# Two attention steps of the first tile moved by one product each, and two of four groups of weight sums formed at the second tile's begin

## The chip, the cores and the metric

The kernel runs on one core of a Trainium2 chip. TensorE (PE) multiplies matrices, VectorE (DVE) and ScalarE (ACT) do elementwise work, GpSimd (POOL) does masks here and issues some DMAs, SyncE (SP) issues most DMAs. Each engine works through its own instructions in order and waits on semaphores for the others. The metric is the device time of one execution in microseconds; lower is better.

## The reference

One layer of a hybrid decoder block on x of 1 x 2048 x 1024 in float32:

```
h = rms_norm(x, norm_g);  u = h @ w_in          # 8704 columns, cut into nine parts
y_c = b_c * conv3(c_c * v_c) * silu(z_c);       y_a = y_c @ w_conv_out
q, k = rms_norm per head (16 and 4 heads of 64)
o = attention(q, k, v, sinks) * silu(z_a);      y_b = o @ w_attn_out
merged = sigmoid(g_a + b) * y_a + sigmoid(g_b + b) * y_b
out = x + merged @ w_out
```

The attention looks back 128 positions, in blocks of 128, and each query head has a learned sink that takes part in the softmax.

## The kernel before, in words

**Tiles and products.** The 2048 positions are worked on in two tiles of 1024 (tile 0 and tile 1), weights on the partitions, positions along the free axis in halves of 512. A projection is cut into units. Each unit (`sunit`, L650) computes a 2 x 2 block of results with seven block products instead of eight, from sums and differences of the blocks of weights and of activations. Every value is held as a rounded high part and a low part, so a product is 4 x 3 = 12 matmuls of 128x128 by 128x512 (`product`, L633; the matmul is L639). The order of the products of a unit is 1, 5, 6, 2, 7, 3, 4: the first fills a bank `X`, which ACT copies to the bank `Y`; the second fills `V`; the third adds into `Y`; then DVE adds `Y` and the kept copy `s5` of `V` into `V`, and only after that the fifth product (weights `th`, `tl`) may go on writing `Y`.

**What sets the order.** All engines run in the order in which the program was written (a manual schedule). The function `run` takes one product after the other and counts them in `tick`; `put(n, f)` places a piece of other work right behind product n. So a number in one of the tables at the head of the file is the number of a product, and one product is the unit in which work is moved. Tile 1 runs k, v, four units of q, eight of conv inputs with four of b, the gates ga and gb, four of z, four of za, then the output projections.

**Attention.** One step is one group of four query heads and one block of 128 queries; there are 32 in a tile, numbered 0 to 31 (step r has key head r // 8 and block r % 8). Step r is placed by STEPS_0[r] for tile 0 and STEPS_1[r] for tile 1, a product number n: SP loads the operands (n - 5, for three late steps n - 6), ACT puts the sinks as a column into the bank of scores (`att_bank` L1237, n - 2), PE forms the scores `s` (L1249 and L1252, n), ACT the exponentials `p` (L1274, n + 1), DVE normalises (n + 2) and transposes within 32 x 32 squares into `f` (n + 2), POOL stores that to HBM (`fd`, L1293) and loads it back in another order (`x`, four DMAs, L1300, n + 4), ACT rounds it to `xh` and `yp` (n + 9), DVE forms the low part `xl` (n + 10) and POOL masks with four selects (L1321, n + 10), PE multiplies with the values into `po` (L1338, n + 13, for two steps n + 14), ACT and DVE sum `po` into `o` (up to n + 15), and SP stores it (`od`, L1358). There is one bank of scores in all.

**Weight sums of w_out.** `wo_sums(n, j)` (L1595) forms for one of four groups of 256 rows of `w_out` the four differences that the last projection needs: behind product n SP loads two pieces of 512 KB into the two buffers of the pool `u` (`wos`, L1601); from n + 5 to n + 7 DVE does four subtractions of 128x512 and SP stores each result of 256 KB in HBM (`wsd`, L1606). They are read again much later. The two `u` buffers serve other loads too, but one group fills both, so a group's loads wait for the stores of the group before it.

**Queues.** SP's DMAs take eight semaphores in turn, and a DMA waits until the one issued eight before it has landed. POOL's DMAs do the same with eight of their own. A wait in such a queue holds all that stands behind it.

Of the kernel before, what the change touches and what calls it, by code (L numbers as in the profile page):

```python
# [27 lines left out]
KP = KC // 2  # L28
# [45 lines left out]

CSUM_AT = (2, 14, 12, 20)
CONV_AT = (3, 0, 0, 0, 1, 2, 3, 8, 8, 4, 7, 8, 5, 11, 9, 2, 5, 9, 11, 12, 15, 16, 15, 17, 14, 12, 11, 13)
WO_SUMS_AT = (8, 17, 26, 35)
WO_AHEAD = 3
THS_AT = 10
HOLD = 10  # L80
STEPS_0 = (60, 63, 71, 74, 78, 85, 92, 95, 99, 104, 110, 115, 121, 128, 131, 136, 139, 142, 146, 149, 152, 155, 159, 162, 165, 170, 173, 176, 181, 184, 187, 192)
STEPS_1 = (53, 57, 63, 69, 72, 77, 84, 87, 93, 98, 104, 111, 114, 118, 125, 129, 132, 136, 139, 142, 145, 148, 153, 158, 161, 164, 168, 171, 175, 178, 181, 184)
Z_AHEAD = (7, 4)
SUM_WAIT = 5
# [41 lines left out]
def block_kernel(  # L126
# [13 lines left out]
    NT = S // T  # L140
# [48 lines left out]
    def hs(q):  # L189
        return slice(q * H, (q + 1) * H)  # L190
# [121 lines left out]
    def sub(o, a, b, eng=None):  # L312
        return (eng or vec).tensor_tensor(out=o, in0=a, in1=b, op=ALU.subtract)
# [568 lines left out]
    tick = [0]  # L882
    at = {}

    def put(n, f):
        at.setdefault(max(n, tick[0] + 1), []).append(f)
# [306 lines left out]
    def att_load(t, j, b):  # L1193
        nm = f"{t}_{j}_{b}"
        gb = t * NB + b
        kz = lows[(j * NB + b) % 2]
        q2 = slot([P, 2, 2, P], F32R, f"q2_{nm}")
        nc.sync.dma_start(
            q2.bitcast(F32).rearrange("p h c x -> p (h c x)"),
            q2d[t][j][:, 2 * b : 2 * b + 2].rearrange("p h c e x -> p (h c e x)"))  # L1200

        kq = slot([P, 2, 2 * P], F32R, f"kq_{nm}")
        for c in range(2):
            nc.sync.dma_start(
                kq[HALVES[c], 1].bitcast(F32).rearrange("p (h x) -> p h x", h=2),
                q2d[t][j][LH, 2 * b : 2 * b + 2, c].rearrange("p h e x -> p h (e x)"))

        blocks = [(t, b - 1, 0, 2)] if b else [(t, 0, 1, 1)]
        if b == 0 and gb > 0:
            blocks.append((t - 1, NB - 1, 0, 1))  # L1210
        for kt, k0, to, n in blocks:
            here, there = slice(to * P, (to + n) * P), slice(k0 * P, (k0 + n) * P)
            nc.sync.dma_start(kq[:, 0, here].bitcast(F32), kd[kt][j, :, 0, there])
            for c in range(2):
                nc.sync.dma_start(kz[HALVES[c], c, here].bitcast(F32), kd[kt][j, HALVES[c], 1, there])
        return q2, kq, kz

    def att_load_v(t, j, b):

        v2 = slot([P, 4, P], F32R, f"v2_{t}_{j}_{b}")
        hb = (t * NB + b) * 2
        v4 = v2.bitcast(F32).rearrange("p n d -> p (n d)")
        src = vd[j, :, hb : hb + 4].rearrange("k n d -> k (n d)")
        nc.sync.dma_start(v4[UH], src)

        pairs = src[:, 0 : 2 * P].unsqueeze(1).to_broadcast([HD, 2, 2 * P])
        (rows, _, cols_) = pairs.ap  # L1230
        pairs = bass.AP(pairs.tensor, pairs.offset, [rows, [P, 2], cols_])
        nc.sync.dma_start(v4[LH].rearrange("p (i x) -> p i x", i=2), pairs)
        return v2

    def att_bank(t, j, b):
        sp = ps_s.tile([P, 2, 2, 2 * P], F32, tag="s", name=f"s{t}_{j}_{b}")
        nc.scalar.copy(sp[:, :, :, 3 * HD : 3 * HD + 1], sinks_of[t, j][:, b // HB, b % HB].unsqueeze(3))  # L1237
        return sp

    def att_scores(t, j, b, ld, sp):  # L1240
        first = t * NB + b == 0
        nm = f"{t}_{j}_{b}"
        q2, kq, kz = ld
        rv = rqs[t, j][:, b // HB, b % HB]
        for h in range(2):
            skip = (2 - h) * HD if first else 0
            keys = slice(h * HD + skip, (h + 3) * HD)
            for c in range(2):
                nc.tensor.matmul(  # L1249
                    sp[:, h, c, skip : 3 * HD], lhsT=q2[:, h, c, :], rhs=kq[:, 0, keys],  # L1250
                    start=c == 0, stop=False)
            nc.tensor.matmul(  # L1252
                sp[:, h, :, skip : 3 * HD], lhsT=kq[:, 1, h * P : (h + 1) * P], rhs=kz[:, :, keys],
                start=False, stop=True)
        sg = sp.rearrange("p h c k -> p (h c) k")
        m = mask_i.unsqueeze(1).to_broadcast([P, G, HD])
        if first:
            vec.copy_predicated(
                sg[:, :, 2 * HD : 3 * HD], m, negc.unsqueeze(1).to_broadcast([P, G, HD]))
            vec.tensor_copy(sg[:, 0:2, HD : 2 * HD], negc.unsqueeze(1).to_broadcast([P, 2, HD]))  # L1260
        else:
            vec.copy_predicated(sg[:, :, 2 * HD : 3 * HD], m, sg[:, :, 0:HD])
        st = small.tile([P, 3, G], F32, tag="st", bufs=4, name=f"st{nm}")
        vec.tensor_reduce(out=st[:, 0], in_=sg[:, :, HD : 3 * HD + 1], axis=AX.X, op=ALU.max)
        vec.scalar_tensor_tensor(
            out=st[:, 1], in0=st[:, 0], scalar=-1.0, in1=rv.rearrange("p h c -> p (h c)"),
            op0=ALU.mult, op1=ALU.mult)
        return sg, st, rv

    def att_exp(t, j, b, got):  # L1270
        sg, st, rv = got
        p = slot([P, G, P + 1], F32, f"p{t}_{j}_{b}")
        for i in range(G):
            nc.scalar.activation(  # L1274
                out=p[:, i, :], in_=sg[:, i, HD : 3 * HD + 1], func=AF.Exp, bias=st[:, 1, i : i + 1],
                scale=rv[:, i // 2, i % 2 : i % 2 + 1], accum_out=st[:, 2, i : i + 1])
        return p[:, :, 0:P], st
# [317 lines left out]
    def wo_sums(n, j):  # L1595
        two = []

        def ld():
            for i in range(2):
                u = upool.tile([P, 2 * H + 2], F32, tag="u", name=f"wos_{j}_{i}")  # L1600
                nc.sync.dma_start(u[:, 0 : 2 * H], w_o[(2 * j + i) * P : (2 * j + i + 1) * P, :])  # L1601
                two.append([u[:, hs(q)] for q in range(2)])

        def out(m, a, b, c):
            sub(a, b, c)
            nc.sync.dma_start(wsd[m, j], a)  # L1606

        put(n, ld)
        put(n + SUM_WAIT, lambda: out(0, two[0][0], two[0][1], two[0][0]))
        put(n + SUM_WAIT + 1, lambda: out(1, two[0][1], two[1][1], two[0][1]))  # L1610
        put(n + SUM_WAIT + 1, lambda: out(2, two[1][1], two[1][1], two[0][0]))
        put(n + SUM_WAIT + 2, lambda: out(3, two[1][0], two[1][0], two[1][1]))
# [57 lines left out]
    for n in range(S // P // 2):  # L1670
        t, c0 = divmod(2 * n * P, T)
# [204 lines left out]
    def attention(t, places):  # L1876
        for r, n in enumerate(places):
            j, b = divmod(r, NB)
            got = {}

            def step(k, f, got=got):
                def g():
                    got[k] = f(got)
                return g

            put(n - 5 - ((t, r) in EARLY_LOADS), step("l", lambda g, j=j, b=b: att_load(t, j, b)))
            put(n + V_, step("v", lambda g, j=j, b=b: att_load_v(t, j, b)))
            put(n - 2, step("k", lambda g, j=j, b=b: att_bank(t, j, b)))
            put(n, step("s", lambda g, j=j, b=b: att_scores(t, j, b, g["l"], g["k"])))
            put(n + 1, step("e", lambda g, j=j, b=b: att_exp(t, j, b, g["s"])))  # L1890
            put(n + 2, step("n", lambda g: att_norm(g["e"])))
            put(n + F_, step("f", lambda g, j=j, b=b: att_flip(t, j, b, g["n"])))
            put(n + B_, step("b", lambda g, j=j, b=b: att_back(t, j, b, g["f"])))
            put(n + X_, step("x", lambda g, j=j, b=b: att_turn(t, j, b, g["b"])))
            put(n + L_, step("w", lambda g: att_low(g["x"])))
            late = int((t, r) in VALUES_LATER)
            put(n + late + O_, step("o", lambda g, j=j, b=b: att_values(t, j, b, g["w"], g["v"])))
            put(n + late + O_ + 1, step("z", lambda g, j=j, b=b: att_out(t, j, b, g["o"])))
            put(n + late + S_, step("t", lambda g, j=j, b=b: att_sum(t, j, b, g["z"])))
# [56 lines left out]
    for t in range(NT):  # L1956
# [5 lines left out]
            t0 += T0_SHIFT  # L1962


        attention(t, [t0 + n for n in (STEPS_0, STEPS_1)[t]])
        if t > 0:
            run(sunit(("k", t), ops, fin_k(t)))
# [25 lines left out]
        zs += [("za", j) + fin_z(t, j, od[t], "za", use_y) for j in range(NJ)]  # L1993
        zs[0][3]()
        if t + 1 == NT:
            for j in range(KP):
                wo_sums(tick[0] + WO_SUMS_AT[j], j)
        if t == 0:
            for j in range(2):
# [151 lines left out]
```

## Time and profile before

| what | value |
|---|---|
| median of 3 runs | 1901.33 us (1898.82 to 1902.93) |
| the profiled execution, its own time | 1901.07 us |
| its span, first to last instruction | 1899.4 us |
| PE busy | 1888.9 us, 99% |
| PE weight loads | 1572.7 us, 83% |
| DVE busy | 1498.6 us, 79% |
| ACT busy | 990.5 us, 52% |
| POOL busy | 608.7 us, 32% |
| granted TensorE clock | 1.000 |
| HBM traffic | 271.09 MB read, 129.25 MB written |

In the rows of a timeline stand the start and the length in microseconds, the engine, the line, the operation, what it writes and reads, the shapes, how many instructions were put together, and in brackets the idle time of the engine before it with what ended it. Matmuls overlap, so a row of 0.61 us of two matmuls does not fill as much time: twelve of them follow each other in 2.7 us. In tile 0 the last attention steps lie between about 545 and 630 us; tile 1 begins near 890 us, its q units run from 928 to 1004 us, its z units start at 1432 us.

### The profile page before, as it was taken

The numbers are of one execution on the slowest core, as the hardware profiler recorded it, in microseconds if no ns is written. First come the engines' busy times: TensorE is split into PE (matmuls) and PEld (weight loads), VectorE is DVE, ScalarE is ACT, GpSimd is POOL, SyncE is SP. The second block draws the span as 40 slices with busy tenths as digits, with TensorE's granted clock in tenths as the row PEclk, the third lists the DMA queues.
The fourth block names the chain that finished last, engine by engine and source line by source line (L and its number), as shares of the span: only waits on it lengthen the run. The fifth ranks groups of instructions, "written<-read, shape, count | busy, mean of one in ns | idle before, by whom it ended". The sixth has DMA issues, their size and how long they took to land.

```text
span 1899.4 us, 27260 instructions
## 1 busy us (share of the span) xinstructions
PE 1888.9 (99%) x8670; PEld 1572.7 (83%) x8670; DVE 1498.6 (79%) x2364; ACT 990.5 (52%) x1967; POOL 608.7 (32%) x846
## 2 busy tenths in 40 slices
PE   9999999999999999999999999999999999999999
PEld 7888888888887888888888888888888888888887
DVE  7989898887777767668799788887778777787754
ACT  7665455456766443434565455556666434444321
POOL 2073435335655000011372344445656000121000
PEclk9999999999999999999999999999999999999999
DMA  8286555568777957895584655567778887779653
GB/s 299 77 238 177 167 169 167 162 189 245 240 229 226 302 197 245 276 279 130 155 233 128 181 175 154 168 206 228 242 235 256 272 319 274 274 194 264 215 175 110
DMA packets 222495, 402.20 MB, mean 212 GB/s; under 512 B 30032, under 2 KB 104784, under 8 KB 212880
## 3 DMA queue, kind: packets, MB, share of 16 engines
q1 hardware_dynamic: 188224, 313.10, 50.6%
q0 software_dynamic: 30528, 78.94, 15.7%
q10 hardware_dynamic: 3600, 8.42, 1.3%
q8 instruction: 69, 1.13, 0.2%
q14 instruction: 74, 0.61, 0.1%
HBM read 271.09 MB, written 129.25 MB: 211 GB/s over the span
## 4 chain that ended last, share of the span: by engine, by line
PE 65%; DVE 2%; DMA 2%; issue 0%; ACT 0%; SPq 0%; DVEq 0%; ACTq 0%
PE Y L639 24%; PE ya L1479 4%; PE Vcv L639 2%; PE Xcv L639 2%; PE Xyb L639 2%; PE Vo L639 2%; PE Xo L639 2%; PE Vyb L639 2%; PE Vza L639 2%; PE Xza L639 2%; PE Xz L639 1%; PE Vz L639 1%; PE po L1338 1%; PE Vga L639 1%; PE Xgb L639 1%; PE Vgb L639 1%
## 5 line engine op out<-in xcount | busy, mean ns | idle before, releaser
L1300 POOL DMA_DIRECT2D x<-fd x256 | 140.0, 554 | 127.0 <-DMA fd<-f 58.1
L1274 ACT ACTIVATE p<-s,st,rq 128x129 f32<-128x129 f32 x256 | 114.2, 458 | 33.2 <-DVE st L275 21.2
L1321 POOL TENSOR_SCALAR_AFFINE_SELECT xh<-xh 64x512 fp32r<-64x512 f32 x64 | 61.0, 953 | 151.4 <-DVE xl L275 103.2
L1293 POOL DMA_DIRECT2D fd<-f x64 | 37.0, 578 | 194.3 <-DVE f L275 169.0
L1562 POOL DMA_DIRECT2D mt<-tha x16 | 13.8, 863 | 254.9 <-DVE tha L275 236.2
L639 PE MATMUL Xcv<-oph,wcv_ah 128*128 128x512 f32 x256 | 78.9, 389 | 0.0
L1321 POOL TENSOR_SCALAR_AFFINE_SELECT yp<-xl 64x512 fp32r<-64x512 f32 x64 | 72.3, 1130 | 3.1
L1321 POOL TENSOR_SCALAR_AFFINE_SELECT xl<-xl 64x512 fp32r<-64x512 f32 x64 | 67.7, 1058 | 4.4
L1321 POOL TENSOR_SCALAR_AFFINE_SELECT yp<-yp 64x512 fp32r<-64x512 f32 x64 | 57.8, 903 | 4.2
L275 DVE TENSOR_TENSOR o<-po,o 64x256 f32<-64x256 f32 x128 | 53.5, 418 | 5.0 <-ACT o L1350 4.1
L275 DVE SCALAR_TENSOR_TENSOR y<-u,cols,y 128x512 f32<-128x512 f32 x64 | 53.6, 837 | 3.7 <-ACT y L1387 2.5
L639 PEld LDWEIGHTS Xcv<-oph,wcv_ah 128*128 128x128 f32 x256 | 47.8, 188 | 9.4
L275 DVE TENSOR_TENSOR p<-p,st 128x512 f32<-128x512 f32 x64 | 50.4, 787 | 3.4
L275 DVE STREAM_TRANSPOSE f<-p 128x512 f32<-128x512 f32 x64 | 45.5, 711 | 8.5 <-DMA fd<-f 5.6
L466 ACT CAST wcv_sh<-wcv_raw 128x1024 fp32r<-128x1024 f32 x16 | 16.9, 1054 | 67.1 <-DVE wcv_raw L275 67.1
L1274 ACT ACTIVATION_READ_ACCUMULATOR p<-s,st,rq 128x1 f32 x256 | 51.3, 200 | 0.0
L1249 PEld LDWEIGHTS s<-kq,q 128*128 128x128 f32 x256 | 46.1, 189 | 5.8 <-ACT s L1237 1.8
L1078 POOL DMA_DIRECT2D q2d<-q_h x64 | 44.3, 692 | 18.9 <-ACT q_h L1073 7.7
L1350 ACT COPY o<-po 64x256 f32<-64x256 f32 x128 | 47.1, 368 | 6.0 <-DMA wpd_yb<-wph_yb 2.2
L2052 POOL DMA_DIRECT2D oc<-ocd x12 | 6.5, 545 | 136.1 <-ACT ophc L306 130.1
L639 PE MATMUL Xcv<-oph,wcv_al 128*128 128x512 f32 x128 | 49.9, 390 | 0.0
L1078 POOL DMA_DIRECT2D q2d<-q_l x64 | 44.2, 690 | 14.7 <-DMA q2d<-q_h 7.5
(711 smaller groups left out, 6409.1 us busy)
## 6 DMA issues: line engine op xcount, KB each, us to landing
gd<-th SPq DMA_DIRECT2D x64, 256.0 KB, 2.8
wcv_raw<-in_w_units SPq DMA_DIRECT2D x16, 1024.0 KB, 5.5
q<-q2d SPq DMA_DIRECT2D x64, 256.0 KB, 5.4
v<-vd SPq DMA_DIRECT2D x128, 128.0 KB, 3.5
fd<-f POOLq DMA_DIRECT2D x64, 256.0 KB, 4.2
x<-fd POOLq DMA_DIRECT2D x256, 64.0 KB, 3.5
th<-gd SPq DMA_DIRECT2D x48, 256.0 KB, 5.0
wga_raw<-in_w_units SPq DMA_DIRECT2D x8, 1024.0 KB, 5.4
```

What stands on the lines that cost most here:

```text
L275: r = f(*args, **kw)
L466: return (lambda: nc.scalar.copy(hi, src), lambda: vec.tensor_tensor(out=lo, in0=src, in1=hi.bitcast(F32), op=ALU.subtract))
L639: nc.tensor.matmul(ps, lhsT=w[:, j, :], rhs=b[:, m, :], start=start and j == 0 and i == 0, stop=j == KP - 1 and i == 2, skip_group_check=n ...
L1078: nc.gpsimd.dma_start(q2d[t][j][half, q * 2 * HB : (q + 1) * 2 * HB, i, e, :], src[HALVES[e]].bitcast(F32).rearrange("p (b x) -> p b x", x ...
L1249: nc.tensor.matmul(sp[:, h, c, skip : 3 * HD], lhsT=q2[:, h, c, :], rhs=kq[:, 0, keys], start=c == 0, stop=False)
L1274: nc.scalar.activation(out=p[:, i, :], in_=sg[:, i, HD : 3 * HD + 1], func=AF.Exp, bias=st[:, 1, i : i + 1], scale=rv[:, i // 2, i % 2 : i ...
L1293: nc.gpsimd.dma_start(fd, f)
L1300: nc.gpsimd.dma_start(x[QUADS[k]], src[k])
L1321: nc.gpsimd.affine_select(out=d4, in_=s4, pattern=[[0, 2], [-32 * sg, 2], [0, G], [-sg, 32]], compare_op=ALU.is_gt if prev else ALU.is_ge, ...
L1338: nc.tensor.matmul(po[:, cs], lhsT=v2[:, kind + h, :], rhs=xx[:, :, h * HD : (h + 1) * HD], start=n == h == 0, stop=n == 2 and h == 1)
L1350: nc.scalar.copy(ov, pov[oth, :, e])
L1479: nc.tensor.matmul(ps, lhsT=w[:, j, cs], rhs=o[:, m, :], start=n == 0 and i == 0, stop=n == KC - 1 and i == 2)
```

## The change

Two tables and one loop are changed. In STEPS_0 step 28 comes one product earlier (181 to 180) and step 30 one product later (187 to 188); the last five steps then stand at 176, 180, 184, 188 and 192. The four groups of w_out's sums were all placed from the first z unit of tile 1 on, behind its products 8, 17, 26 and 35. Now groups 0 and 1 are placed from tile 1's begin on, behind products 5 and 13 (in k's and v's units), and groups 2 and 3 from the first z unit on, behind products 8 and 44.

```diff
-WO_SUMS_AT = (8, 17, 26, 35)
+WO_SUMS_AT = (5, 13, 8, 44)
...
-STEPS_0 = (..., 170, 173, 176, 181, 184, 187, 192)
+STEPS_0 = (..., 170, 173, 176, 180, 184, 188, 192)
...
+        if t + 1 == NT:
+            for j in range(2):
+                wo_sums(tick[0] + WO_SUMS_AT[j], j)
         attention(t, [t0 + n for n in (STEPS_0, STEPS_1)[t]])
...
         if t + 1 == NT:
-            for j in range(KP):
+            for j in range(2, KP):
                 wo_sums(tick[0] + WO_SUMS_AT[j], j)
```

On POOL, at the end of tile 0's attention, before the change (`3_2`, `3_3` and `3_4` are steps 26, 27 and 28; the last number is the buffer's):

```order
L1300 DMA x_3_3_5716<-fd_3_3_5653 32x4x128 x4
L1321 AFFINE_SELECT xh_3_2_5771<-xh_3_2_5771 64x512
L1321 AFFINE_SELECT yp_3_2_5773<-yp_3_2_5773 64x512
L1321 AFFINE_SELECT yp_3_2_5773<-xl_3_2_5772 64x512
L1321 AFFINE_SELECT xl_3_2_5772<-xl_3_2_5772 64x512
L1293 DMA fd_3_4_5821<-f_3_4_5819 128x512
L1300 DMA x_3_4_5894<-fd_3_4_5821 32x4x128 x4
L1321 AFFINE_SELECT xh_3_3_5886<-xh_3_3_5886 64x512
```

The same place in the changed kernel:

```order
L1300 DMA x_3_3_5716<-fd_3_3_5653 32x4x128 x4
L1293 DMA fd_3_4_5777<-f_3_4_5775 128x512
L1321 AFFINE_SELECT xh_3_2_5768<-xh_3_2_5768 64x512
L1321 AFFINE_SELECT yp_3_2_5770<-yp_3_2_5770 64x512
L1321 AFFINE_SELECT yp_3_2_5770<-xl_3_2_5769 64x512
L1321 AFFINE_SELECT xl_3_2_5769<-xl_3_2_5769 64x512
L1300 DMA x_3_4_5849<-fd_3_4_5777 32x4x128 x4
L1321 AFFINE_SELECT xh_3_3_5894<-xh_3_3_5894 64x512
```

Step 28's store now stands ahead of step 26's four selects; its loads stay between the selects of steps 26 and 27.

On SP, in k's, v's and q's units of tile 1 (`wq` are q's weights, `krd` and `krb` the store and the spread loads of the keys' scales), before:

```order
L437 DMA wq_0_raw<-in_w_units 128x2048
L437 DMA wq_1_raw<-in_w_units 128x2048
L1143 DMA krd_104<-krt_8938 32x32 x4
L1152 DMA krb_0_0_8980<-krd_104 64x512 x2
L437 DMA wq_2_raw<-in_w_units 128x2048
L1152 DMA krb_1_1_9036<-krd_104 64x512 x2
```

and in the changed kernel:

```order
L437 DMA wq_1_raw<-in_w_units 128x2048
L1606 DMA wsd<-wos_0_8764 128x512 x2
L1606 DMA wsd<-wos_1_8766 128x512 x2
L1143 DMA krd_104<-krt_8950 32x32 x4
L1601 DMA wos_0_8977<-in_w_out 128x1024
L1601 DMA wos_1_8979<-in_w_out 128x1024
L1152 DMA krb_0_0_8996<-krd_104 64x512 x2
L437 DMA wq_2_raw<-in_w_units 128x2048
L1152 DMA krb_1_1_9052<-krd_104 64x512 x2
L1152 DMA krb_0_1_9102<-krd_104 64x512 x2
L1606 DMA wsd<-wos_0_8977 128x512 x2
```

The first group's loads stand ahead of the rows shown, its stores ahead of `krd`; the second group's two loads now stand between `krd` and the first `krb`.

On DVE, between q's first and second unit of tile 1, in the changed kernel:

```order
L275 SCALAR_TENSOR_TENSOR q_0_0_0_l<-q_0_0_0_t,gqk,q_0_0_0_h 128x512
L275 TENSOR_TENSOR wos_0_8977<-wos_0_8977 128x512
L275 TENSOR_TENSOR k_1_1_t<-k_1_1_t,krb_1_1_9052 128x512
L275 TENSOR_TENSOR wq_1_d<-wq_1_raw,wq_1_d 128x512
L275 TENSOR_TENSOR q_0_1_1_t<-Y,s5q_0_9083 128x512
L275 TENSOR_TENSOR wos_0_8977<-wos_1_8979,wos_0_8977 128x512
L275 TENSOR_TENSOR wos_1_8979<-wos_1_8979,wos_0_8977 128x512
L275 TENSOR_TENSOR k_1_1_l<-k_1_1_t,k_1_1_h 128x512
```

Before, the three `wos` rows were not there and the others followed each other; the group's fourth subtraction comes five rows further on. All four stand ahead of the second unit's `Vq`.

More of the change, by code (lines that the diff above doesn't have):

```diff
@@ L80 @@
 HOLD = 10
-STEPS_0 = (60, 63, 71, 74, 78, 85, 92, 95, 99, 104, 110, 115, 121, 128, 131, 136, 139, 142, 146, 149, 152, 155, 159, 162, 165, 170, 173, 176, 181, 184, 187, 192)
+STEPS_0 = (60, 63, 71, 74, 78, 85, 92, 95, 99, 104, 110, 115, 121, 128, 131, 136, 139, 142, 146, 149, 152, 155, 159, 162, 165, 170, 173, 176, 180, 184, 188, 192)
 STEPS_1 = (53, 57, 63, 69, 72, 77, 84, 87, 93, 98, 104, 111, 114, 118, 125, 129, 132, 136, 139, 142, 145, 148, 153, 158, 161, 164, 168, 171, 175, 178, 181, 184)
```

## The prediction

> **What bounds the kernel now.** I read the page first, then the waits of TensorE (PE), then the chain of waits around each of them, then the timelines of the engines named there.
>
> ```profile
> span 1899.4 us, 27260 instructions
> ...
> PE 1888.9 (99%) x8670; PEld 1572.7 (83%) x8670; DVE 1498.6 (79%) x2364; ACT 990.5 (52%) x1967; POOL 608.7 (32%) x846
> ```
>
> TensorE is busy for all but 10.5 us of the span. The change removes no matmul, so only those idle microseconds are to be won, while a new pause of TensorE is lost whole. The waits of TensorE (line, who released it, us in total, times, longest) say where they are:
>
> ```profile
> PE s L1249 <- ACT s L1237: 1.4, 1, 1.4
> ...
> PE po L1338 <- POOL yp L1321: 0.8, 1, 0.8
> PE Y L639 <- DVE zs L275: 0.8, 1, 0.8
> PE po L1338 <- DMA gd<-th: 0.6, 1, 0.6
> PE po L1338 <- POOL xl L1321: 0.3, 1, 0.3
> ```
>
> The two `po` waits on POOL and the `s` wait lie among the last attention steps of tile 0, the `Y` wait in tile 1's z stage, where w_out's sums are formed. They make 0.8 + 0.3 + 1.4 + 0.8 = 3.3 us, or 0.17% of the time: all that the change can win.
>
> **Attention, first wait.** In POOL's timeline (start, length, idle time and its releaser in brackets), with two rows of VectorE (DVE) and two of PE:
>
> ```profile
> 562.14 1.31 POOL L1321 TENSOR_SCALAR_AFFINE_SELECT xh<-xh 64x512 fp32r<-64x512 f32 x1 [3.70 <-DVE st L275]
> ...
> 566.76 0.58 POOL L1293 DMA_DIRECT2D fd<-f  x1
> 573.49 2.19 POOL L1300 DMA_DIRECT2D x<-fd  x4 [6.14 <-issue]
> 575.68 0.76 POOL L1321 TENSOR_SCALAR_AFFINE_SELECT xh<-xh 64x512 fp32r<-64x512 f32 x1
> ...
> 579.16 0.58 POOL L1293 DMA_DIRECT2D fd<-f  x1
> ```
> ```profile
> 562.86 0.71 DVE L275 STREAM_TRANSPOSE f<-p 128x512 f32<-128x512 f32 x1
> ...
> 583.33 0.71 DVE L275 STREAM_TRANSPOSE f<-p 128x512 f32<-128x512 f32 x1 [3.40 <-DMA fd<-f]
> ```
> ```profile
> 578.42 0.51 PE L1338 MATMUL po<-yp,v 128*128 128x256 f32 x2 [0.79 <-POOL yp L1321]
> ...
> 589.33 0.47 PE L1249 MATMUL s<-kq,q 128*128 128x192 f32 x2 [1.37 <-ACT s L1237]
> ```
>
> The reader sees POOL finish step 26's four selects (562.14 to 566.8), issue step 28's store `fd`, stand still until that has landed, issue its four loads `x`, and only then begin step 27's selects at 575.68, for which TensorE waits at 578.42. One product of twelve matmuls takes 2.72 us:
>
> ```profile
> 599.33 2.72 PE Y L639 x12
> ```
>
> With step 28 one product earlier its `f`, now at 562.86, comes at best at 562.86 - 2.72 = 560.1, inside POOL's idle 3.70 us; its store stands ahead of step 26's selects now. The landing (566.76 to 573.49, 6.7 us) then runs beside them: 560.2 + 6.7 = 566.9. DVE does step 28's three operations first, about 1.6 us (0.71 for the transpose, the rest from it by size), so the selects end at some 568.4, the loads are issued by 570.6, and step 27's selects begin 5 us earlier than 575.68. TensorE's wait needs 1.1 of that: **-1.11** (0.79 and 0.32). Should `f` not come earlier at all, the store goes out at 563.6, the selects follow, and step 27's begin at about 572: enough too. If DVE's reordering eats more, the wait stays: bounds -1.11 and 0.
>
> **Second wait.** Step 29's store goes out at 579.16 because it stands behind step 27's selects. Step 30's transpose waits until 583.33 for a slot that this store holds; behind it DVE is late for weights, ScalarE (ACT) for a cast, and behind that cast in ACT's order the sink column of step 31 is late, for which TensorE waits 1.37 at 589.33. All that comes 5 us earlier, while step 30 itself is one product later and its transpose stands behind that weight work. **-1.37**; if the single bank of scores, which step 30 now holds a product longer, is free too late, 0.
>
> **What is late next.** TensorE reaches the following stage 2.48 us earlier. The moved step's value product also comes one product later, and the store of its sums falls behind two other rows in SP's queue:
>
> ```profile
> 624.21 0.37 SPq L1358 DMA_DIRECT2D od<-o  x1
> ```
> ```profile
> 634.39 0.75 ACT L1350 COPY o<-po 64x256 f32<-64x256 f32 x2 [2.20 <-DMA wpd_yb<-wph_yb]
> ```
> ```profile
> 637.50 0.70 DVE L275 TENSOR_TENSOR Vz<-s5z,Y 128x512 f32<-128x512 f32 x1
> ```
> ```profile
> 639.52 0.61 PE L639 MATMUL Y<-oph,wz_th 128*128 128x512 f32 x2
> ```
>
> SP stands at 624.21 until the sums exist; the loads and stores of weights behind it (`wp_yb`, `wpd_yb`) hold ACT at 634.39, ACT holds DVE, and DVE's `Vz`, which ends at 638.20, must precede the product at 639.52. That is 1.32 us of slack. If those DMAs keep their times, TensorE, 2.48 early, stands 2.48 - 1.32 = **+1.2** here. If they follow TensorE, nothing; if SP's queue comes half a product later (1.3), +2.5. I take 1.2, because a DMA row (634.39) released ACT.
>
> **w_out's sums at tile 1's begin.** Each group is two loads of 512 KB, four subtractions on DVE and four stores of 256 KB. One subtraction (ns, minimum/median/maximum):
>
> ```profile
> L275 DVE TENSOR_TENSOR wos<-wos x8: 679/685/692, 1475.7 to 1554.5; 128x512 f32<-128x512 f32 x8
> ```
>
> The first group falls into this stretch (us, then busy us of PE, PEld, DVE, ACT, POOL; clock, DMA share, GB/s):
>
> ```profile
> 905.00:925.00 20.00, 20.00 (x94) 16.60 (x93) 15.67 (x35) 10.02 (x19) 1.97 (x4) 1.00 0.18 60
> ```
>
> DVE idles 4.3 us and the DMA engines are at 0.18, so its 2.7 us of DVE and 2 MB cost 0; without that cover 2.7. The second group stands between q's first and second unit on DVE:
>
> ```profile
> 942.14 0.69 DVE L275 TENSOR_TENSOR k_t<-k_t,krb 128x512 f32<-128x512 f32 x1 [0.54 <-DMA krb<-krd]
> ...
> 956.09 0.69 DVE L275 TENSOR_TENSOR k_l<-k_t,k_h 128x512 fp32r<-128x512 f32 x1 [1.58 <-ACT k_h L306]
> ...
> 957.30 0.69 DVE L275 TENSOR_TENSOR Vq<-s5q,Y 128x512 f32<-128x512 f32 x1
> ```
> ```profile
> 958.32 0.61 PE L639 MATMUL Y<-oph,wq_th 128*128 128x512 f32 x2
> ```
>
> The product at 958.32 overwrites what `Vq` reads, and `Vq` ends at 957.99: 0.33 us of slack. Four subtractions at about 0.65 from start to start put 2.6 us ahead of it. The idle 0.54 takes the first; the idle 1.58 doesn't help, since it ends with an ACT result that itself follows DVE's transposes. So 2.6 - 0.54 - 0.33 = **+1.7**. Should the 1.58 absorb too: 0.15; should TensorE's lead up to here (1.11 + 1.37 - 1.2 = 1.28) come on top, because DVE doesn't follow it: 3.0.
>
> **z stage.** The chain of waits before TensorE's `Y` wait:
>
> ```profile
> 1481.88 9.29 DMA wsd<-wos
> ...
> 1501.32 7.82 DMA cr<-ocd
> ...
> 1509.24 0.69 DVE cr L275
> 1509.93 0.53 DVE wza_d L275
> 1510.46 0.68 DVE zs L275
> ```
>
> A store of these very sums, held in flight 9.29 us, delays SP's next loads; 27 us later DVE stands on `cr`. The second group, whose loads and stores made this, is gone from here: **-0.75** (the wait's exact length by the timeline), 0 if `cr` is late for other reasons. The third group, now first, keeps the old place of the first; the last, moved nine products on, costs DVE 2.7 us where TensorE showed no wait: 0.
>
> **Sum**: -1.11 - 1.37 + 1.2 + 1.7 - 0.75 = -0.33. The profiled execution took 1901.07 (1899.4 of span and 1.67 around it), 0.26 below the median 1901.33 of the three runs, so 1900.74, or **1900.7 us**.
>
> **Rivals.** (1) *The costs don't come*: DMAs follow TensorE at 634.39 and DVE's idle time absorbs the subtractions; -3.23 + 0.15 gives 1898.0. For it: DVE idles 1.58 right ahead of the tight place. Against: that idle is a link of the chain, not a gap in it. (2) *Keys come late, slower*: SP's queue now reads krd, two w_out loads, krb.
>
> ```profile
> 924.44 1.75 SPq L1143 DMA_DIRECT2D krd<-krt  x4
> 927.26 1.30 SPq L1152 DMA_DIRECT2D krb<-krd  x2
> ```
> ```profile
> 935.20 0.68 DVE L275 TENSOR_TENSOR k_t<-k_t,krb 128x512 f32<-128x512 f32 x1
> 936.83 0.69 DVE L275 TENSOR_TENSOR Vq<-s5q,Y 128x512 f32<-128x512 f32 x1 [0.94 <-ACT k_h L306]
> ```
> ```profile
> 939.28 0.61 PE L639 MATMUL Y<-oph,wq_th 128*128 128x512 f32 x2
> ```
>
> From issue to landing the w_out loads and stores took (first row, us, minimum/median/maximum), and krb (second):
>
> ```profile
> DMA to landing us min/median/max: 2.0/5.7/9.3
> ```
> ```profile
> DMA to landing us min/median/max: 2.6/7.1/8.0
> ```
>
> The second load needs the buffer of the first group, so its last store's landing. That store goes out by 924.4; at 9.3 it lands at 933.7, krb follows at 934.1 and lands 7.1 later at 941.2: 6.0 after DVE wants it at 935.20. `Vq` then ends at 943.5 against 939.28 (+4.2), and at the second unit at 957.99 + 2.06 + 6.0 = 966.05 against 962.5 (+3.5): 7.7 in place of 1.7, so 1906.8. It decides from a landing over some 3.3 us on (935.2 - 7.1 - 0.4 - 924.4). Against it: the DMA share of 0.18, where landings near 2.0 are likely.
> [...]
> (3) *The attention part doesn't pay*: both waits stay, TensorE isn't early, the 1.2 isn't due; +1.7 - 0.75 gives 1902.0. For it: SP and slots are reordered too, and the step before the last now follows its neighbour by four products only.
>
> **Chances.** Forecast 0.55, costs absent 0.20, attention not paying 0.15, late keys 0.10. Faster means below 1897.5, slower above 1905.1 (0.2% of the median, about what a measurement of this kernel can tell from no change; the three runs span 4.1 us). With that scatter rival 1 gives 0.09 of faster and the forecast 0.04: 0.13. Late keys give 0.08 of slower, the others 0.04: 0.12. The same: 0.75. The range goes from rival 1 less a little scatter, 1897.2, to short of late keys, 1905.4; the forecast's own is 1898.7 to 1902.7.
>
> **What would show it.** Right: no `po` and `s` wait near 577 and 589, nor a `Y` wait near 1511; new waits of about 1 us before the `th` products near 638 and nearly 2 near 957. Wrong: no wait at 957 (DVE had room); a wait at both of q's first units, with DVE on krb (late keys); `po` waits still there.

## The result

| | median | range | ratio to before, 95% interval |
|---|---|---|---|
| before | 1900.53 us, 20 runs | from 1897.24; one run of 2319.31 aside, up to 1903.30 | |
| changed | 1907.28 us, 20 runs | 1901.99 to 1910.88 | 1.0035 (1.0028 to 1.0043) |

The change makes the kernel 0.35% slower, 6.75 us between the medians. The prediction said 1900.7 with 1897.2 to 1905.4 and gave "slower" 0.12, so it was wrong in sign and in range. Its slower rival (keys late) had given 1906.8.

The profiled execution of the changed kernel was one of the fastest of the twenty, 1902.20 us. Its page begins:

```profile
span 1900.5 us, 27275 instructions
...
PE 1888.3 (99%) x8670; PEld 1572.0 (83%) x8670; DVE 1498.8 (79%) x2364; ACT 990.0 (52%) x1967; POOL 604.8 (32%) x846
```

The waits of TensorE in it (line, who released it, us in total, times, longest):

```profile
PE Y L639 <- DVE q_t L275: 2.6, 1, 2.6
PE Y L639 <- DVE Vz L275: 2.0, 1, 2.0
...
PE Y L639 <- DVE Vq L275: 1.5, 1, 1.5
...
PE po L1338 <- POOL xl L1321: 0.2, 1, 0.2
```

The waits that the change was to remove are gone: no `s` wait, 0.2 left of the `po` waits on POOL, no `zs` wait. The two that the forecast named have come: `Vz` (near 637, forecast 1.2, here 2.0) and `Vq` (near 960, forecast 1.7, here 1.5). A third was not forecast: `q_t`, 2.6, near 943. This execution alone would almost have borne out the forecast; the median doesn't. So the same kernel was run again, and that time a long execution was profiled, 1913.07 us. Its span and its waits of TensorE:

```profile
span 1911.4 us, 27275 instructions
```
```profile
PE Y L639 <- DVE Vq L275: 8.1, 1, 8.1
PE Y L639 <- DVE Vz L275: 2.2, 1, 2.2
...
PE po L1338 <- POOL xl L1321: 1.4, 2, 0.8
PE Y L639 <- DVE q_t L275: 1.0, 1, 1.0
```

The `Vq` wait is 8.1 us here in place of 1.5. SP's timeline (start, length, what), SP's own waits and the chain of waits ahead of TensorE's say what came late:

```profile
943.37 5.70 SPq L1606 DMA_DIRECT2D wsd<-wos  x3
949.17 5.63 SPq L1152 DMA_DIRECT2D krb<-krd  x2
```
```profile
SPq L1606 <- DVE wos L275: 8.1, 2, 4.4
```
```profile
949.67 2.78 SPq L1152
...
952.50 11.38 DMA krb<-krd
...
963.98 0.70 DVE k_t L275
...
967.47 0.69 DVE k_l L275
...
968.68 0.69 DVE Vq L275
...
969.42 5.48 PE Y L639 x12
```

The last pair of the keys' spread loads (`krb`) stands on SP behind three stores of w_out's second group (`wsd`), which SP can't issue before DVE has formed them (8.1 us of SP's waits there). Before the change all the `krb` loads behind the first pair went out in one piece:

```profile
934.57 4.19 SPq L1152 DMA_DIRECT2D krb<-krd  x6
```

They were through by 938.8. Now the pair's first load is issued 10.4 us later (949.17), that issue alone takes 3.28 us, where the eight `krb` issues took at most 0.97 before (why so long is not shown), and the last load is issued at 952.50 and takes 11.38 us; DVE's `k_t` waits for it, `Vq` stands behind `k_t` on DVE, and TensorE behind `Vq`.

The last row shows a second loss. Twelve matmuls take 5.48 us, where they took 2.72 before. By stretch (us, then busy us and instruction count of PE, PEld, DVE, ACT, POOL; then the granted clock, the DMA share, GB/s):

```profile
640.00:645.00 5.00, 5.00 (x17) 3.94 (x16) 4.01 (x7) 0.00 (x0) 0.00 (x0) 0.66 0.99 375
...
965.00:970.00 5.00, 0.58 (x1) 0.50 (x2) 3.43 (x7) 3.05 (x5) 3.50 (x7) 0.50 0.87 247
970.00:975.00 5.00, 5.00 (x14) 3.87 (x13) 4.29 (x7) 2.91 (x5) 4.54 (x8) 0.52 0.88 273
975.00:980.00 5.00, 5.00 (x24) 4.14 (x23) 4.51 (x7) 2.30 (x4) 0.85 (x2) 1.00 0.51 129
```

Behind each of the two long waits TensorE's granted clock is lower for a while (0.66 from 640 to 645, 0.50 and 0.52 from 965 to 975), and with 5.00 us busy it starts 17 and 14 matmuls instead of the 24 of the last row. One wait of before, which the prediction did not show, lies in code that the change doesn't touch, and is in neither execution of the changed kernel:

```profile
PE Y L639 <- DVE th L275: 1.0, 1, 1.0
```

The balance of the long execution against the profile of before: new waits 8.1 + 2.2 + 1.0 = 11.3; `po` waits on POOL 1.4 in place of 1.1; the `s`, `zs`, `th` and the `po` wait on a DMA gone, 1.4 + 0.8 + 1.0 + 0.6 = 3.8; the slow product 5.48 - 2.72 = 2.8 and seven matmuls fewer from 640 to 645, 7 x 0.227 = 1.6. Together 11.3 + 0.3 - 3.8 + 4.4 = 12.2, and the span has grown by 1911.4 - 1899.4 = 12.0. The agreement is closer than the sum deserves: it leaves out two waits of 0.5 us at the kernel's begin, which differ from one execution to the next. By the two pages TensorE's idle time has grown from 10.5 to 19.3, by 8.8 (the waits above and these 1.0), and its busy time from 1888.9 to 1892.1, by 3.2, so the 4.4 for the clock is some 1 us too much.

### The profile page after: what moved, and what is told of

The parts are those of the page before. It is cut to its first block, busy times and chain, and to the rows that moved or that the text cites. A ratio compares the mean times of both kernels' runs of the same rounds, so it can differ in the third digit from the quotient of the medians.

```text
span 1900.5 us, 27275 instructions
## 1 busy us (share of the span) xinstructions
PE 1888.3 (99%) x8670; PEld 1572.0 (83%) x8670; DVE 1498.8 (79%) x2364; ACT 990.0 (52%) x1967; POOL 604.8 (32%) x846
## 4 chain that ended last, share of the span: by engine, by line
PE 94%; DVE 2%; DMA 2%; issue 1%; ACT 0%; POOL 0%; SPq 0%; DVEq 0%; ACTq 0%; POOLq 0%
PE Y L639 34%; PE ya L1479 5%; PE Vcv L639 5%; PE Xcv L639 5%; PE po L1338 2%; PE Vyb L639 2%; PE Vb L639 2%; PE Vgb L639 2%; PE Xgb L639 2%; PE Xb L639 2%; PE Xyb L639 2%; PE Vo L639 2%; PE Xo L639 2%; PE Vza L639 2%; PE Xza L639 2%; PE Vga L639 2%
```

## The experiments

All are timed against the kernel before on the same chip.

| run | median, us | ratio to before (95%) |
|---|---|---|
| the change again | 1907.15 | 1.0043 (1.0026 to 1.0060) |
| steps 28 and 30 only | 1902.31 | 1.0011 (1.0003 to 1.0020) |
| w_out's groups only | 1904.91 | 1.0028 (1.0017 to 1.0039) |
| first group early only | 1899.84 | 0.9999 (0.9990 to 1.0008) |
| groups only, second group's stores later | 1901.94 | 1.0007 (0.9998 to 1.0015) |
| the same without that group's subtractions | 1899.40 | 0.9998 (0.9989 to 1.0006) |
| groups only, second group at 20 | 1902.54 | 1.0008 (0.9999 to 1.0017) |
| step 28 only | 1898.34 | 0.9986 (0.9977 to 0.9995) |
| step 30 only | 1904.99 | 1.0021 (1.0012 to 1.0029) |
| steps 28 and 30, step 30's store later | 1900.35 | 1.0003 (0.9994 to 1.0012) |
| the change, these five stores later | 1900.68 | 1.0002 (0.9993 to 1.0011) |
| step 28 and the first group early | 1896.22 | 0.9981 (0.9972 to 0.9990) |

**The change again, unaltered.** 

> The changed kernel unaltered, run again, because its profiled execution took 1902.20 at a granted clock of 1.000 while the median of its 20 runs was 1907.28 at clocks of mostly 0.996 to 0.999. Theory K (keys): w_out's second group holds the keys' spread loads krb up in SP's queue, TensorE waits at q's first two units, in the profiled execution 2.6 and 1.5 us, in most others longer, and a lower granted clock follows from there; median 1906 to 1908, ratio 1.0035. Rival S (steps): the longer part of the loss is in tile 0, where TensorE waits 2.0 us at 635; same median. Rival C (chip): the lower clock has nothing to do with the change and the difference goes away: ratio 1.000 to 1.001, about 1901.5.

1907.15 us, so the loss and the lower clock belong to the change (against theory C; K and S both have this time): its granted clock lay between 0.996 and 1.000 over seven runs, and that of before at 0.999 or 1.000 in all 25 beside it. The profile is the one shown above.

**The two halves of the change.** 

```diff
-STEPS_0 = (..., 176, 181, 184, 187, 192)
+STEPS_0 = (..., 176, 180, 184, 188, 192)
```

> Only the attention steps 28 and 30 moved, w_out's sums as before. From the two profiles: waits of 1.1 and 1.4 us go, 0.2 comes at 589 and 2.0 at 635, the 0.75 wait at 1511 stays. Theory K: within 0.5 us of before, ratio 0.9995 to 1.0005, clock 1.000. Rival S: 1904 to 1907, ratio 1.002 to 1.0035. Rival C: as theory K.

And w_out's part of the diff alone, the steps as before:

> Only w_out's groups moved (0 and 1 to tile 1's begin, 2 and 3 behind products 8 and 44 of the z stage), the attention steps as before. Theory K: the whole loss is here, 1905 to 1908, ratio 1.003, waits of TensorE at q's first two units with DVE on krb. Rival S: 1900 to 1903, ratio 1.000 to 1.001. Rival C: 1901 to 1903.

Both halves lose: 0.11% and 0.28%, together about the whole. The groups are the larger part, as theory K said; that the steps would cost nothing was wrong, though they cost less than theory S had them. In the run with the groups alone the wait is at q's second unit; at the first, where theory K had one too, there is none:

```profile
PE Y L639 <- DVE Vq L275: 4.8, 1, 4.8
```

**The first group alone.** 

```diff
-WO_SUMS_AT = (8, 17, 26, 35)
+WO_SUMS_AT = (5, 17, 26, 35)
...
+            for j in range(1):
+                wo_sums(tick[0] + WO_SUMS_AT[j], j)
```

> Before, but for w_out's first group alone, which moves to product 5 of tile 1; the groups 1, 2, 3 stay behind products 17, 26, 35 of the z stage. Its stores lie ahead of the keys' loads, but no second group's loads do. Theory K: no wait at q's units, 1899.5 to 1901, ratio 0.9990 to 1.0005. Rival: any load and store at tile 1's begin is enough (the stores hold SP, then krd and krb): a wait of 1 us or more at q's units and 1903 or more.

0.9999: the first group's loads, subtractions and stores at tile 1's begin cost nothing that can be measured. So the loss is the second group's, or that of the new places of the third and fourth; the next three runs keep these places and lose at most 0.08%.

**The second group: the queue, the bytes or DVE.** Three runs tell these apart, all with the steps as before. In the first the four stores come two products after the last subtraction, behind the last `krb` pair on SP, and nothing else is altered:

```diff
             sub(a, b, c)
-            nc.sync.dma_start(wsd[m, j], a)
+            if j == 1:
+                put(n + 9, lambda: nc.sync.dma_start(wsd[m, j], a))
+            else:
+                nc.sync.dma_start(wsd[m, j], a)
```

> The run with only w_out's groups moved, but the second group's four stores are issued two products after its last subtraction, so that on SP they stand behind the last pair of the keys' spread loads krb; its loads and its subtractions stay where the change put them. Attention steps as before. Theory Q (queue): the 4.8 us wait at q's second unit comes from SP holding the last krb pair behind three stores that themselves wait for DVE; with the stores behind it the wait is at most 1.7 us and the ratio 0.9995 to 1.001. Rival B (bytes): the group's loads in flight make the krb landings long (7.7 to 8.2 in the middle instead of 7.1); the wait stays at 3 us or more, ratio 1.002 or more. Rival D (DVE): the wait is that of four subtractions ahead of Vq, 1.7, ratio 1.001.

In the second the subtractions of that group are left out as well:

```diff
+            if j != 1:
+                sub(a, b, c)
```

> The run with the second group's stores behind the last krb pair, without the four subtractions of that group: its loaded pieces are stored as they are, so w_out's differences of the second group are left out. Theory D (DVE): the 1.5 us that were left at q's second unit are the four subtractions ahead of Vq; without them no wait of over 0.3 there, 1899.5 to 1900.8, ratio 0.9990 to 1.0003. Rival B (bytes): they are the loads' and stores' traffic on the krb landings; the wait stays at 1 us or more, ratio 1.0005 to 1.001.

In the third the whole group is put behind the last `krb` pair:

```diff
-WO_SUMS_AT = (5, 13, 8, 44)
+WO_SUMS_AT = (5, 20, 8, 44)
```

> The run with only w_out's groups moved, but the second group is put behind product 20 of tile 1 instead of 13: its loads, subtractions and stores all stand behind the last krb pair on SP, and its subtractions lie behind the second unit's Vq on DVE. Theory Q: no wait on krb, none of 1 us or more at q's units, 1899 to 1901.5, ratio 0.9990 to 1.0008. Rival B: the store and load traffic of two groups anywhere near q's units is too much, 1903 or more. Rival D: the four subtractions are ahead of the third unit's Vq instead, a wait of 1 to 2 us there, ratio 1.0005 to 1.001.

With the stores later, SP's `krb` loads behind the first pair go out in one piece again:

```profile
935.22 4.28 SPq L1152 DMA_DIRECT2D krb<-krd  x6
```

TensorE's waits at q's units with the stores later (first fence), also without the subtractions (second), and with the group at 20 (third):

```profile
PE Y L639 <- DVE Vq L275: 1.5, 1, 1.5
```
```profile
PE Y L639 <- DVE q_t L275: 0.3, 1, 0.3
```
```profile
PE Y L639 <- DVE Vq L275: 1.1, 1, 1.1
PE Y L639 <- DVE q_t L275: 0.5, 1, 0.5
```

Four stores moved in SP's order take the `Vq` wait from 4.8 to 1.5 and the loss from 0.28% to 0.07%, with intervals that don't meet: that is theory Q. The 1.5 that stays goes with the four subtractions, as theory D has it, and there is no `Vq` wait without them; the two ratios (1.0007 and 0.9998) fit, but their intervals overlap, so this rests on the waits. The bytes of the group's loads are not the cause: the 1 MB stood where the change put it in both. The stores' own bytes moved along with them, so this doesn't part the late issue of the last `krb` pair from its longer landing (issue to landing of `krb` at most 10.2 us with the groups alone, 8.6 with the stores later, 8.0 before); the issue is by far the larger part, 949.6 against 938.6 for the last one. Put at 20 the group meets no late `krb` but stands ahead of the third unit's `Vq`, with 1.1 and 0.5 us of waits.

**Which step loses.** 

```diff
-STEPS_0 = (..., 176, 181, 184, 187, 192)
+STEPS_0 = (..., 176, 180, 184, 187, 192)
```

> Before, with step 28 alone one product earlier. Theory H (step 30 makes the new wait): the waits at 577 and 587 go (1.1 and 1.4), TensorE's wait near 636 is at most 1.3, ratio 0.9985 to 0.9997. Rival L (lead): TensorE's lead alone makes the wait near 636 of 2.0 to 2.6, with a lower clock behind it; ratio 0.9995 to 1.001. Rival N: the wait at 587 stays, since it follows from step 30; ratio 0.9993.

```diff
-STEPS_0 = (..., 176, 181, 184, 187, 192)
+STEPS_0 = (..., 176, 181, 184, 188, 192)
```

> Before, with step 30 alone one product later. Theory H: the wait of 2 us or more near 636 with a lower clock behind it is here, while the wait at 577 stays: ratio 1.001 to 1.002. Rival L: no wait of over 0.5 near 636, ratio 0.9995 to 1.0005. Rival N: the wait at 587 goes with this step: 1.4 less than otherwise.

Step 28 alone gains 0.14%, some 2.7 us, and step 30 alone loses 0.21%, some 4 us (2.1 and 4.6 between the medians). That is theory H, if a little above its 1.002 for step 30, and against L and N: with step 28 alone there is neither a wait near 636 nor one near 587. With step 28 alone POOL begins step 27's selects here, against 575.68 before:

```profile
567.50 0.76 POOL L1321 TENSOR_SCALAR_AFFINE_SELECT xh<-xh 64x512 fp32r<-64x512 f32 x1
```

TensorE has neither the two `po` waits nor the `s` wait there, nor any near 636. With step 30 alone:

```profile
PE Y L639 <- DVE Vz L275: 4.0, 1, 4.0
...
PE s L1249 <- ACT s L1237: 0.7, 1, 0.7
PE po L1338 <- POOL xl L1321: 0.3, 1, 0.3
...
PE po L1338 <- POOL yp L1321: 0.3, 1, 0.3
```

The cause was followed in the run with both steps. SP's timeline (first fence), ACT's (second), the chain of waits (third):

```profile
622.32 0.37 SPq L1435 DMA_DIRECT2D zin<-yd  x1
627.58 0.37 SPq L1358 DMA_DIRECT2D od<-o  x1
628.05 1.86 SPq L339 DMA_DIRECT2D wp_yb<-in_w_units  x4
```
```profile
636.25 0.74 ACT L1350 COPY o<-po 64x256 f32<-64x256 f32 x2 [6.22 <-DMA wpd_yb<-wph_yb]
```
```profile
630.43 5.80 DMA wpd_yb<-wph_yb
...
639.37 0.71 DVE Vz L275
...
640.12 4.43 PE Y L639 x12
```

SP stands from 622.7 to 627.6 for the sums of step 30, with loads and stores of `wp_yb` and `wpd_yb` behind that store. Before, it stood at the same store until 624.21. So the store is 3.4 us later than before though TensorE is earlier; the `wp_yb` loads behind it begin 2.2 us later (628.05 against 625.82) and the first `wpd_yb` store 0.7 (630.43 against 629.69), to be 5.80 us in flight. ACT, which waits for a `wpd_yb` store before it copies `po`, stands 6.22 us in place of 2.20, and `Vz` ends at 640.08 in place of 638.20. The twelve matmuls behind the wait take 4.43 us, 1.7 more than 2.72, and the granted clock of this execution is 0.999, against 1.000 before.

**Step 30's store later.** 

```diff
-        nc.sync.dma_start(od[t]..., o)
+        if (t, j, b) == (0, 3, 6):
+            put(tick[0] + 2, keep_sums)
+        else:
+            keep_sums()
```

> The run with only the two attention steps moved, but the store od of step 30's sums is issued two products later, so that on SP the four loads wp_yb of w_conv_out's pieces and two of the stores wpd_yb stand ahead of it. Theory Q (queue): SP's stand of about 5 us for step 30's sums, which became 2 to 4 us of TensorE's wait near 637 through ACT's wait on a wpd_yb store, is gone: that wait is at most 1.3 us, 1897.5 to 1899.5, ratio 0.9980 to 0.9995. Rival L (lead): the wait is that of TensorE's 2.5 us lead on unmoved transfers, 2 us stay, ratio 1.000 to 1.001. Rival A (ACT): step 30's copies of po stand on ACT ahead of the work that is late; the wait stays at 2 us or more and ACT is not released by a wpd_yb store.

```profile
622.24 5.16 SPq L339 DMA_DIRECT2D wp_yb<-in_w_units  x4
...
631.52 3.25 SPq L1988 DMA_DIRECT2D ocd<-zin  x2
```
```profile
PE Y L639 <- DVE Vz L275: 1.1, 1, 1.1
```

The stand for step 30's sums is gone and the wait falls from 2.6 to 1.1, as theory Q said. The time, 1.0003, is above the forecast 0.9980 to 0.9995, and its interval overlaps that of the run without this edit, so the store's part rests on the waits: 1.1 here and 1.5 in the next run, against 2.0 to 2.6 in the three profiles with both steps and the store in its place. SP's stand comes back in part, spread over the four `wp_yb` loads (5.16 us in place of 1.86) and two `ocd` stores; SP's waits put 3.0 us of it down to a `po` product, 1.6 before.

By the rows the 1.1 that is left is a sum: TensorE comes here 2.5 us earlier than before (637.00 against 639.52), `Vz` ends 0.1 earlier (638.10 against 638.20), and the slack was 1.3. TensorE's lead alone makes no wait, though: with step 28 alone it comes 3.9 us earlier (635.63) and finds none, because SP is past its store 3.5 us earlier too (620.67 against 624.21). So the queue is shown as the cause of about half of this wait, and the other half comes from transfers that don't follow TensorE; no run takes away what still holds them.

**Five stores.** 

> The whole change, with five stores on SP issued later and nothing else altered: step 30's od two products later, and the second group's four wsd two products after its last subtraction, behind the last krb pair. Theory Q (queue): nearly all of the change's loss of 0.35 to 0.43% is these five stores holding SP; what stays is the subtractions ahead of Vq (1.5 to 1.7) and a rest near 637 of at most 1.3, against the waits that the change removes: 1899.5 to 1902, ratio 0.9995 to 1.0012. Rival B (bytes): the group's loads and TensorE's lead keep the wait at q's units at 3 us or more: 1904 or more, ratio 1.002 or more.

The edit is that of the two store experiments together, on the whole change. The time is 1900.68, ratio 1.0002 against 1.0035 of the change. TensorE's waits:

```profile
PE Y L639 <- DVE Vz L275: 1.5, 1, 1.5
PE Y L639 <- DVE Vq L275: 1.5, 1, 1.5
```

Those are the two new waits of the forecast, 1.2 and 1.7, and its result, no change. The agreement is in part luck, since of the waits that were to go 0.7 us of `s` and 0.7 of `po` near 590 are still in this profile, which is of the longest of the eleven executions. No matmul, subtraction or load was moved for it: five stores in SP's order were the loss.

**What is worth keeping.** 

```diff
-WO_SUMS_AT = (8, 17, 26, 35)
+WO_SUMS_AT = (5, 17, 26, 35)
...
-STEPS_0 = (..., 176, 181, 184, 187, 192)
+STEPS_0 = (..., 176, 180, 184, 187, 192)
```

> Step 28 one product earlier and w_out's first group alone at tile 1's begin (product 5), the other three groups as before. If the parts add: the 2.1 to 2.7 of step 28 and the 0 to 0.9 of the z stage's wait, 1897 to 1898.5, ratio 0.9981 to 0.9990. Rival: the lead of 2.5 us meets an unmoved transfer in tile 1's begin or the z stage and a part of it is lost, 1899 to 1900, ratio 0.9993 or more.

```profile
span 1894.5 us, 27270 instructions
```
```profile
PE Y L639 <- DVE th L275: 0.9, 1, 0.9
```

1896.22 us, 0.19% below before and faster than both kernels. The parts add. The `th` wait that is left is in code that no kernel here alters; it stands in the profile of before with 1.0, and not in that of the change.

## Why the prediction was wrong, step by step

**First and second wait (-1.11, -1.37): right for step 28 alone, less in the whole change.** Both belong to step 28. Step 27's selects begin 8 us earlier than before when step 28 alone is moved, where 5 were forecast. With step 30 moved too, 0.2 to 0.7 us of `po` waits on POOL came back near 590 and `s` waits of 0.2 to 1.0 in some of the profiles; nothing of that was priced.

**What is late next (+1.2): the path was right, the size was not.** The prediction named step 30's store behind two other rows of SP's queue and ACT's wait on `wpd_yb`, and gave 2.5 for a queue half a product late. It then took 1.2, "because a DMA row (634.39) released ACT". That was not enough: the DMA itself is issued from behind the store that step 30 makes late. Measured: 2.0 to 2.6 with both steps, 4.0 with step 30 alone. In the run with both steps `Vz` ends 1.9 us later than before, where the forecast had 0, and TensorE comes 2.0 earlier, where it had 2.5: 2.0 - 1.3 + 1.9 = 2.6. In the change's own profile `Vz` ends 0.6 earlier and TensorE comes 3.9 earlier, 1.0 of it because the `th` wait isn't there: 3.9 - 1.3 - 0.6 = 2.0.

**w_out's second group (+1.7): the term was right and incomplete.** The four subtractions ahead of `Vq` cost 1.5, in the change's own profile and with the stores out of the way. The step that failed most is here: the edit was priced on DVE alone, and SP's stand for the group's stores was put at nothing. The row of SP's order with the group's first store behind the third `krb` pair stood in the part on the change, and what the last pair behind it would wait for was not worked out. It costs 3.3 us more in the run with the groups alone (4.8 - 1.5), and 6.6 in the long execution of the whole change (8.1 - 1.5).

**The rival of late keys (0.10, 1906.8): right in kind, wrong in place, and dismissed for a wrong reason.** That its time lies near the measured 1907.28 is luck, since it had other waits and no clock. It took the first `krb` pair to be late behind the loads of w_out. In the changed kernel DVE's `k_t` takes the first pair without standing idle, and the second pair holds it 3.28 us (profile of the change, DVE's timeline):

```profile
933.11 0.68 DVE L275 TENSOR_TENSOR k_t<-k_t,krb 128x512 f32<-128x512 f32 x1
...
943.66 0.69 DVE L275 TENSOR_TENSOR k_t<-k_t,krb 128x512 f32<-128x512 f32 x1 [3.28 <-DMA krb<-krd]
```

The late ones are the second and, in the long execution and with the groups alone, the last. Why the second is later in the change than with the groups alone or with the five stores moved (waits of 2.6 and 1.0 us against at most 0.2) was not tested. The rival was held unlikely by "the DMA share of 0.18", which is that of 905 to 925; the loads run later, and the rows of before for that time read

```profile
925.00:935.00 10.00, 10.00 (x50) 8.24 (x49) 6.27 (x10) 5.14 (x12) 5.67 (x10) 1.00 0.61 146
935.00:945.00 10.00, 10.00 (x46) 8.29 (x45) 6.92 (x11) 4.31 (x8) 7.68 (x13) 1.00 1.00 352
```

with the DMA share (the number before the last) at 0.61 and then at its full value.

**The z stage (-0.75): the wait goes, but not for the reason given.** The store in flight for 9.29 us is the first group's last, and what SP holds for it are the second group's loads (profile of before, first two rows; the first group alone early, third row):

```profile
1481.88 0.47 SPq L1606 DMA_DIRECT2D wsd<-wos  x1
...
1485.25 6.27 SPq L1601 DMA_DIRECT2D wos<-in_w_out  x2
```
```profile
1484.55 1.09 SPq L1601 DMA_DIRECT2D wos<-in_w_out  x2
```

With the first group alone moved the second stays where it was, its loads go out in 1.09 us and the wait is gone. No `zs` wait stands in any of the nine profiles with the first group moved. With it in its old place the wait is 0.2 to 0.9 us and once absent (step 30's store later), so 0.75 is near the upper end of what it was worth.

**The clock: not thought of.** Every new wait was priced at its own length. Behind the waits of 2.2 and 8.1 us in the long execution and of 2.6 us with both steps, the matmuls took 1.6, 2.8 and 1.7 us longer.

**The sum.** Two terms were too small, the second group's (1.7; waits of 1.5 to 8.1 us at `Vq`) and what is late next (1.2; 2.0 to 2.6), and behind both stand stores that hold SP's queue (behind the second term in about half of its size); the clock that fell behind some of these waits was in no term. By the change's own profiled execution the forecast would have missed by 1.5 us: the late `krb` loads (DVE waits 3.3 us for them here, 8.2 in the long execution) and the clock (0.996 to 1.000 in the twenty) vary from one execution to the next, and this one, with no lower clock, was near the fast end.

## What to carry to other kernels

When work is moved, list for every queue it is moved into what stands behind it there, and treat a store as a wait: a store of a result that isn't formed yet holds each load behind it (here three of them put a `krb` load 10.4 us later). A transfer that ended a wait is not a fixed time; look at what its issue stood behind. A new wait of TensorE can cost more than its length (2.2, 2.6 and 8.1 us here cost 1.6, 1.7 and 2.8 more), and one profiled execution near the fast end of the runs says little of the middle (1902.20 against a median of 1907.28).

## What was not expected of the hardware

**The clock fell behind some short waits.** In the long execution of the change it was lower behind the waits of 2.2 and 8.1 us, by the rows shown with the result. With the groups alone it was 0.94 from 955 to 965, the stretch of the 4.8 us wait. The executions with waits of 2.6 us (both steps) and 4.0 us (step 30 alone) have 0.999 over the whole. In the profile of the change it stayed at 1.00 behind the waits of 2.0 and 2.6 us and that of 1.5; with the five stores later, where two waits are 1.5, it is 1.000 over the whole. So the length of the wait alone does not decide it: 2.2 us was followed by a lower clock, 2.6 us in the change's profile was not. What does decide it is not shown.

It fell during the wait of 8.1 us (0.50 from 965 to 970, where TensorE goes on at 969.42 only), but behind that of 2.2 us not before TensorE had gone on: from 635 to 640, the stretch of that wait, TensorE was busy for 2.76 us and the clock was 1.00, from 640 to 645 it was 0.66. Twelve matmuls of 128x512 then took 5.48 us behind the wait of 8.1 and 4.43 behind that of 2.6, in place of 2.72. The run with only the second group's stores later shows the clock lower behind three pieces of idle time, 2.1 us in all, among the `po` waits (0.7, 1.1 and 0.3; columns as above; 5.00 - 3.10 = 1.9 of the 2.1 lie in the first row):

```profile
575.00:580.00 5.00, 3.10 (x14) 1.99 (x12) 1.73 (x4) 4.54 (x12) 4.81 (x7) 1.00 0.80 219
580.00:585.00 5.00, 4.79 (x15) 3.90 (x16) 1.63 (x3) 0.00 (x0) 1.21 (x3) 0.66 0.61 199
```

Without that group's subtractions the pieces are 0.2, 1.1 and 0.3, 1.6 in all, and the granted clock of that execution is 0.999; where in it the clock was lower is not shown.

**One load took over 11 us.** The `krb` loads of 128 KB took at most 8.0 us from issue to landing before, and at most 11.7 in the long execution of the change (the last one 11.38, by the chain above), with a DMA share of 0.98 from 955 to 960 and 0.86 from 960 to 965; what held it is not shown.
